# Four input projections of a decoder layer on one core: one 512-column matmul over both parts of x in place of two 256-column passes

## The chip, the cores and the metric

One core of a Trainium2 chip. The metric is the device time of one call in microseconds (us), the median of repeated runs. TensorE, VectorE, ScalarE and GpSimd are called PE, DVE, ACT and POOL, as the profile calls them; SP is the queue that issues most of the DMAs.

## What is computed

A decoder layer for 256 tokens of 1024 channels in float32: RMS norm, one input projection that feeds three branches, a merge with sigmoid gates, an output projection, a squared-ReLU MLP and a final norm. The branches: A is causal attention with 8 heads, B is attention with 8 heads over the 64 keys that an index score selects for each query, C is a short convolution with a gated linear recurrence, multiplied by a GeLU gate.

```python
proj = xn @ w_in
(qa, ka, va, qb, kb, vb, qi, ki, wi, xc, yc, gates) = jnp.split(proj, IN_OFFSETS, axis=-1)
y_a = moba_attention(heads_a(qa), heads_a(ka), heads_a(va), rel_bias[:, :N_HEADS_A])
y_b = dsa_attention(heads_b(qb), heads_b(kb), heads_b(vb), qi, ki, wi, rel_bias[:, N_HEADS_A:])
y_c = rg_lru(causal_depthwise_conv(xc, conv_w, conv_b), ...) * jax.nn.gelu(yc)
# dsa: score[t,s] = sum_h wi[t,h] * relu(qi[t,h] . ki[s]); the 64 best s of each t are kept
x = x + (g0 * (y_a @ w_pa) + g1 * (y_b @ w_pb) + g2 * (y_c @ w_pc)) @ w_o
x = x + jnp.square(jax.nn.relu(rms_norm(x) @ w_up)) @ w_down
```

## The kernel before, in words

Float32 products are made of two rounded parts: every operand is split into a high part (a copy into fp32r by ACT) and the rest (a subtraction by DVE), and a product is three passes, high by high, high by low and low by high. Weights come as 73 tiles of 128x2048, each as two halves of 128x1024; a half is loaded into `raw` (L142), copied into `hi` on ACT (L134) and subtracted into `lo` on DVE (L135). There are five places for `raw` and six each for `hi` and `lo`.

The stages, in the order of the program: index queries, index key and weights (`qi`, `ki`, `wi`) in an order written out by hand (from L327); the index score over 8 heads (L438 to L453) and the selection, eight rounds of MAX8 and MATCH_REPLACE8 for each half of the tokens (L455 to L471); the branch C input `xc` (L506 to L511), its convolution, its gates (`ps_ri`) and the scan; its other input `yc` (L543 to L559); `vb`, `kb`, `qb` and attention B; `va`, `ka`, `qa` and attention A; gates, projections of the branches, `w_o`; the MLP. Outside the parts that are written out by hand, the order of each engine's instructions is made when the kernel is built, by a planner that goes by priorities (program order, unless `tc.high_priority(offset)` puts a block ahead by so many places) and by its own estimate of time; the chip then runs each queue in that fixed order.

Tiles come from pools. All tiles of one tag share that tag's places, and a new tile gets a place when an earlier one is released. The tags that matter here: `acc`, three banks of PSUM of 512 columns, for all projections; `t1`, four places of 128x256, for every temporary of up to 256 columns (`tmp`, L92); `t2`, seven places of 128x512; `u4`, eight places of 128x1024.

In `t1` lie, in program order: some small tiles of the first stage, the rectified index logits `rl` of the first token half (L444), the sixteen tiles `mr` of the selection (L464), and in each attention the tiles `b2` (B only), `z` and `e` of the first token half (L607 to L617). In `t2` lie among others `rl` of the second token half and `y1`, `y2` of the GeLU (L546). In `u4` lie the projected keys and queries, the values, the attention outputs of A, the merged products `mh` and `ml`, and the gain `gf` of the final norm (L775), which is loaded from memory and depends on nothing else.

The projections `xc`, `yc`, `kb`, `qb`, `ka`, `qa` are each 512 features by 256 tokens and are made in two steps `h` of 256 features. A step is `fmajor` (L191): for each chunk of 128 features, three passes of eight matmuls of 256 columns, two chunks side by side in one bank. Then `times` (L416) multiplies the bank by the row `rr` of norm factors on DVE, straight from PSUM, with a high priority. `wide` (L203) is used by the MLP only: eight matmuls of 512 columns (the high weights against both parts of x) and eight of 256 (the low weights against the high part).

`pair_keys` (L255) makes for a pair of heads the copies of the keys: four by ACT, two subtractions and two small copies `keysh` by DVE. `both_parts` (L262) makes two small copies of the queries and two subtractions on DVE. They run once for the index keys (`pair_keys` alone) and once for each of the four pairs of both attentions.

Of the kernel before, what the change touches and what calls it, by code (L numbers as in the profile page):

```python
# [22 lines left out]
AF = mybir.ActivationFunctionType  # L23
# [5 lines left out]
P = 128  # L29
KW = 72  # L30
S = 256
# [20 lines left out]
EVAC = 3000  # L52
# [7 lines left out]
def layer(ctx, tc, x, xf, wts, kiwi, small, wri, rel_bias, onehot, gfin, out):  # L60
    nc = tc.nc
# [15 lines left out]
    def f(ap):  # L77
        return ap.bitcast(F32)

    def acc_tile(name):  # L80
        return pacc.tile([P, 512], F32, tag="acc", name=name)

    def att_tile(name, tag):
        return patt.tile([P, 512], F32, tag=tag, name=name, bufs=1 if tag == "y" else 2)

    def big(name, dt=F32):
        return u4.tile([P, 1024], dt, tag="u4", name=name)

    def side(name, dt=F32):
        return u4.tile([P, 1024], dt, tag="side", name=name, bufs=SIDE)  # L90

    def tmp(name, n, dt=F32):  # L92
        if n <= 256:
            return t1.tile([P, 256], dt, tag="t1", name=name)[:, :n]
        return t2.tile([P, 512], dt, tag="t2", name=name)[:, :n]
# [37 lines left out]
    def split(hi, lo, raw):  # L133
        nc.scalar.activation(hi, raw, AF.Copy)  # L134
        nc.vector.tensor_sub(lo, raw, f(hi))  # L135

    def load(i):

        r = []
        for j in range(2):  # L140
            raw = wp.tile([P, 1024], F32, tag="raw", name=f"raw{i}_{j}", bufs=RAW_BUFS)
            nc.sync.dma_start(raw, wts[i, :, j * 1024:(j + 1) * 1024])  # L142
            r.append((raw, *(wp.tile([P, 1024], F32R, tag=p, name=f"{p}{i}_{j}", bufs=HL_BUFS) for p in ("hi", "lo"))))
        return r
# [4 lines left out]
    def weights():  # L149

        i = next_tile[0]
        next_tile[0] += 1
        if i not in loaded:
            with tc.high_priority(offset=AHEAD):
                loaded[i] = load(i)
                for raw, hi, lo in loaded[i]:
                    split(hi, lo, raw)
        return [w[1:] for w in loaded.pop(i)]
# [32 lines left out]
    def fmajor(ps, w, xx, nk=8, ks=None, cs=(0, 1)):  # L191

        part, ks = ks is not None, ks or range(nk)
        pv = ps.rearrange("p (c t) -> p c t", c=2)
        for c in cs:
            ww = [z.rearrange("p (k c) -> p k c", c=P) for z in w[c]]
            for n, (a, b) in enumerate(PASSES):
                for k in ks:
                    nc.tensor.matmul(pv[:, c, :], ww[a][:, k, :], xx[b][:, k, :],  # L199
                                     start=(n == 0 and k == 0 and (c == 0 or not part)),  # L200
                                     stop=(n == 2 and k == nk - 1 and (c == 1 or not part)))

    def wide(ps, w, x2, ks=range(8)):  # L203

        wh, wl = (z.rearrange("p (k c) -> p k c", c=P) for z in w)
        for k in ks:
            nc.tensor.matmul(ps, wh[:, k, :], x2[:, k], start=(k == 0), stop=False)  # L209
        for k in ks:  # L210
            nc.tensor.matmul(ps[:, :S], wl[:, k, :], x2[:, k, 0], start=False, stop=(k == 7))  # L211
# [12 lines left out]
    xn2 = const.tile([P, 8, 2, S], F32R, name="xn2", tag="xn2")  # L224
    xn = xnh, xnl = xn2[:, :, 0, :], xn2[:, :, 1, :]
# [21 lines left out]
    keys2 = const.tile([P, 2, 2, S], F32R, name="keys2")  # L247
    keysh = const.tile([P, 2, 2, P], F32R, name="keysh")
# [6 lines left out]
    def pair_keys(i, k):  # L255
        for j, r in enumerate(rows):
            for o in rows:
                nc.scalar.activation(keys2[o, i, j, :], k[r], AF.Copy)
            nc.vector.tensor_sub(keysl[r, i, j, :], k[r], f(keys2[r, i, j, :]))
            nc.vector.tensor_copy(keysh[r, i, j, :], f(keys2[r, i, j, :P]))  # L260

    def both_parts(qq, qh, q, scale):  # L262

        for j, r in enumerate(rows):
            nc.vector.tensor_copy(qq[r, j], f(qh[r]))
            nc.vector.scalar_tensor_tensor(qq[rows[1 - j], j], q[r], scale, f(qh[r]), op0=ALU.mult, op1=ALU.subtract)

    ps_q = [acc_tile("ps_qi0"), acc_tile("ps_qi1")]
# [7 lines left out]
    rr = const.tile([P, S], F32, name="rr")  # L276
# [50 lines left out]
    with tc.manual_schedule(engines=ENGINES):  # L327
# [58 lines left out]
        for o in (0, 64):  # L386
            nc.vector.tensor_mul(ki2[o:o + 64], ps_kw[:64, :S], rr[:64])
        pair_keys(0, ki2)
        nc.vector.tensor_copy(wif[64:], ps_kw[64:, :S])

# [22 lines left out]
        nc.vector.tensor_scalar(wi[:, t, :], pt[:, t * 64:t * 64 + 8], r1[t], r1[t], op0=ALU.mult, op1=ALU.mult)  # L413


    def times(dst, ps, row):  # L416

        with tc.high_priority(offset=EVAC):
            nc.vector.tensor_mul(dst, ps.rearrange("p (c t) -> p c t", c=2), row[:, None, :].to_broadcast([P, 2, S]))

    def project_f(name):

        dst = big(name).rearrange("p (c t) -> p c t", c=4)
        for h in range(2):
            ps = acc_tile(f"ps_{name}{h}")
            fmajor(ps, weights(), xn)
            times(dst[:, 2 * h:2 * h + 2, :], ps, rr)
        return dst

    def pair_logits(qh, ql, qq, i, name):  # L430
# [9 lines left out]
    for c in range(4):  # L440
        ls = pair_logits(qi[:, c, :], qil[:, c, :], qiq[:, c], 0, f"i{c}")
        for t in range(2):
# [3 lines left out]
            for j in range(2):  # L446
                h = 2 * c + j
                r = rl[:, j * n:(j + 1) * n]
                w = wi[:, t, h:h + 1]
# [56 lines left out]
    xp = wk.tile([P, 4, S + 3], F32, name="xp", tag="bias")  # L506
    nc.gpsimd.memset(xp[:, :, :3], 0.0)
    for h in range(2):
        ps = acc_tile(f"ps_xc{h}")
        fmajor(ps, weights(), xn)  # L510
        times(xp[:, 2 * h:2 * h + 2, 3:], ps, rr)  # L511
    xc = side("xc").rearrange("p (c t) -> p c t", c=4)
    for c in range(4):
        w = [sp[:, C_CW + 4 * c + i:C_CW + 4 * c + i + 1] for i in range(4)]
# [7 lines left out]
    for c in range(4):  # L522
        ps = att_tile(f"ps_ri{c}", "t")
# [17 lines left out]
        nc.vector.tensor_tensor_scan(hs[:, c, :], av[:, c, :], it[:, c, :], 0.0, op0=ALU.mult, op1=ALU.add)  # L541
    yc = [side("ych", F32R).rearrange("p (c t) -> p c t", c=4), side("ycl", F32R).rearrange("p (c t) -> p c t", c=4)]
    for h in range(2):  # L543
        ps = acc_tile(f"ps_yc{h}")
        fmajor(ps, weights(), xn)
        y1 = tmp(f"y1{h}", 512)  # L546
        y2 = tmp(f"y2{h}", 512)
        times(y1.rearrange("p (c t) -> p c t", c=2), ps, rr)
        nc.scalar.activation(y2, y1, AF.Square)
        nc.vector.tensor_scalar(y2, y2, 0.044715, 1.0, op0=ALU.mult, op1=ALU.add)  # L550
        nc.vector.tensor_mul(y2, y2, y1)
        nc.scalar.activation(y2, y2, AF.Tanh, scale=GELU_C)
        nc.vector.scalar_tensor_tensor(y2, y2, 1.0, y1, op0=ALU.add, op1=ALU.mult)
        hv = hs[:, 2 * h:2 * h + 2, :].rearrange("p c t -> p (c t)")
        nc.vector.scalar_tensor_tensor(y2, y2, 0.5, hv, op0=ALU.mult, op1=ALU.mult)
        ch = yc[0][:, 2 * h:2 * h + 2, :].rearrange("p c t -> p (c t)")
        cl = yc[1][:, 2 * h:2 * h + 2, :].rearrange("p c t -> p (c t)")
        nc.scalar.activation(ch, y2, AF.Copy)
        nc.vector.tensor_sub(cl, y2, f(ch))  # L559
# [21 lines left out]
    def attention(q, k, v, h0, masks, name, pool):  # L581
# [3 lines left out]
        def pair(c):  # L585
            pair_keys(c % 2, k[:, c, :])
            qh, ql = queries(f"qh{name}{c}"), queries(f"ql{name}{c}", 3)
            ql, qq = ql[:, 0], ql[:, 1:]
            nc.scalar.activation(qh, q[:, c, :], AF.Copy, scale=0.125)
            nc.vector.scalar_tensor_tensor(ql, q[:, c, :P], 0.125, f(qh[:, :P]), op0=ALU.mult, op1=ALU.subtract)  # L590
            both_parts(qq, qh[:, P:], q[:, c, P:], 0.125)
            return qh, ql, qq
# [66 lines left out]

    vb = project_v("vb")  # L660
    kb = project_f("kb")
    qb = project_f("qb")
    yb = attention(qb, kb, vb, NH, kmask, "b", const)
    va = project_v("va")
    ka = project_f("ka")
    qa = project_f("qa")
    ya = attention(qa, ka, va, 0, None, "a", u4)
# [55 lines left out]
    for d2 in range(2):  # L723
        mm.append(gate(2, d2))
        w = weights()
# [4 lines left out]
    for d2 in range(2):  # L730
        w = weights()
# [8 lines left out]
    with tc.manual_schedule(engines={ET.PE}):  # L740
        w = weights()
        for t in range(2):
            project(0, 0, t, ya, ga[0], w)
        w = weights()
# [3 lines left out]
        for h in range(2):  # L748
            w = weights()
# [4 lines left out]
        w = weights()  # L754
# [3 lines left out]
        w = weights()  # L758
# [5 lines left out]
        w = weights() + weights()  # L764
# [71 lines left out]
    for t in range(2):  # L836
        v = sm.tile([P, 1], F32, name=f"v2{t}", tag="v")
        nc.vector.tensor_scalar(v, ssq_of(xt[t], f"n2{t}"), 1.0 / DM, EPS, op0=ALU.mult, op1=ALU.add)
        r = tiny_.tile([P, 1], F32, name=f"r2{t}")
# [5 lines left out]
    for t in range(2):  # L845
# [28 lines left out]
        r = sm.tile([P, 1], F32, name=f"rf{t}", tag="rf")  # L874
# [114 lines left out]
```

## Time and profile before

| | |
|---|---|
| median of 3 runs | 450.44 us (449.99 to 450.52) |
| the profiled execution | 450.61 us |
| its span on the core | 448.8 us |
| PE / weight loads / DVE / ACT busy | 98% / 86% / 78% / 60% of the span |
| weights and inputs read | 81.1 MB, 185 GB/s over the span |

The span runs from the first to the last instruction of the core; some 1.8 us of the profiled execution's time lie around it. Busy times of PE are those of pipelined matmuls whose ends are modelled, so the distance from one start to the next says what a matmul costs.

### The profile page before, as it was taken

To read this page: it belongs to the slowest core of one execution; us is meant where nothing else is said; L and a number is where in the kernel's file an instruction comes from. 1 tells how busy PE (TensorE), PEld (TensorE's weight loads), DVE (VectorE), ACT (ScalarE), POOL (GpSimd) and SP (SyncE) were. 2 spreads that over 40 slices of the span, in tenths; PEclk is the share of its full clock that TensorE was granted. 3 is DMA by queue.
4 is the path that set the end of the run, shared out by engine and by line. 5 is a ranking of instruction groups with operands and counts; after the bars stand their busy time and mean duration, and the time that the engine had idled before them with its cause. 6 is when DMAs were issued, how large, how long until landed. Compare 5 with 4: busy or idle time off the path is not lost.

```text
span 448.8 us, 6931 instructions
## 1 busy us (share of the span) xinstructions
PE 440.0 (98%) x2482; PEld 384.8 (86%) x2482; DVE 349.6 (78%) x687; ACT 267.7 (60%) x459; POOL 24.1 (5%) x61
## 2 busy tenths in 40 slices
PE   7999999999999999999999999999999999999994
PEld 7999899989988888888888888888888888888884
DVE  6799999999999999985888587666666666666646
ACT  6848496964467888675644466544444444444453
POOL 4820100000010100000000000000000000000000
PEclk9999999999999999999999999999999999999999
DMA  7998767436764462565555645465665566565202
GB/s 243 371 271 289 251 177 235 144 101 211 236 192 155 140 211 84 192 198 162 188 185 188 229 153 182 149 198 188 195 191 194 191 189 195 187 203 184 85 0 93
DMA packets 23838, 83.39 MB, mean 186 GB/s; under 512 B 2987, under 2 KB 3020, under 8 KB 23804
## 3 DMA queue, kind: packets, MB, share of 16 engines
q1 hardware_dynamic: 22608, 80.00, 54.6%
q0 software_dynamic: 960, 2.88, 2.3%
q8 instruction: 19, 0.31, 0.3%
q14 instruction: 15, 0.12, 0.1%
q10 hardware_dynamic: 236, 0.08, 0.1%
HBM read 81.11 MB, written 1.83 MB: 185 GB/s over the span
## 4 chain that ended last, share of the span: by engine, by line
PE 88%; DMA 4%; POOL 3%; DVE 2%; ACT 1%; issue 1%; SPq 0%; ACTq 0%; DVEq 0%; POOLq 0%
PE pd L815 19%; PE ps_g L219 15%; PE ps_up L209 13%; PE ps_p L219 7%; PE ps_up L211 7%; PE po L219 5%; DMA raw<-wts 3%; PE ps_qa L199 3%; PE ps_qb L199 3%; PE ps_kb L199 3%; PE ps_ka L199 3%; PE ps_va L219 2%; PE ps_vb L219 2%; DVE lo L135 1%; DMA x<-xf 1%
## 5 line engine op out<-in xcount | busy, mean ns | idle before, releaser
L135 DVE TENSOR_TENSOR lo<-raw,hi 128x1024 fp32r<-128x1024 f32 (+1 forms) x146 | 174.5, 1207 | 59.1 <-ACT hi L134 58.6
L134 ACT ACTIVATE hi<-raw 128x1024 fp32r<-128x1024 f32 (+1 forms) x146 | 149.8, 1045 | 93.1 <-issue 19.6
L209 PE MATMUL ps_up<-x,hi 128*128 128x512 f32 x256 | 64.7, 393 | 0.2 <-DVE x L186 0.2
L209 PEld LDWEIGHTS ps_up<-x,hi 128*128 128x128 f32 x256 | 46.7, 188 | 9.3 <-DVE x L186 0.4
L219 PE MATMUL ps_g<-hi,xn 128*128 128x512 f32 x192 | 53.7, 392 | 0.0
L815 PE MATMUL pd<-hi,hl 128*128 128x512 f32 (+1 forms) x128 | 49.5, 387 | 0.0
L815 PE MATMUL pd<-lo,hh 128*128 128x512 f32 (+1 forms) x128 | 49.4, 386 | 0.0
L815 PE MATMUL pd<-hi,hh 128*128 128x512 f32 (+1 forms) x128 | 49.1, 387 | 0.0
L219 PEld LDWEIGHTS ps_g<-hi,xn 128*128 128x128 f32 x192 | 35.6, 188 | 6.8
L211 PEld LDWEIGHTS ps_up<-x,lo 128*128 128x128 f32 x256 | 35.3, 190 | 2.7
L211 PE MATMUL ps_up<-x,lo 128*128 128x256 f32 x256 | 36.2, 282 | 0.0
L219 PE MATMUL ps_g<-lo,xn 128*128 128x512 f32 x96 | 30.2, 392 | 0.0
L815 PEld LDWEIGHTS pd<-lo,hh 128*128 128x128 f32 x128 | 24.0, 188 | 5.0
L815 PEld LDWEIGHTS pd<-hi,hh 128*128 128x128 f32 x128 | 24.0, 188 | 4.5
L815 PEld LDWEIGHTS pd<-hi,hl 128*128 128x128 f32 x128 | 24.1, 188 | 4.4
L802 ACT ACTIVATE hh<-z 128x512 fp32r<-128x512 f32 x16 | 10.1, 631 | 29.1 <-DVE z L800 29.1
L219 PEld LDWEIGHTS ps_g<-lo,xn 128*128 128x128 f32 x96 | 17.9, 188 | 3.6
L803 DVE TENSOR_TENSOR hl<-z,hh 128x512 fp32r<-128x512 f32 x16 | 11.1, 691 | 9.8 <-ACT hh L802 9.8
L168 POOL TENSOR_TENSOR ssq_n<-q_n 128x1 f32<-128x1 f32 x2 | 0.4, 192 | 277.6 <-ACT scr_n L166 277.6
L796 DVE TENSOR_TENSOR z<-ps_up,u 128x256 f32<-128x256 f32 x32 | 13.4, 418 | 0.0
L684 ACT ACTIVATE g<-ps_g,rh 128x512 f32<-128x512 f32 x12 | 8.2, 684 | 7.0 <-PE ps_g L219 7.0
L795 ACT ACTIVATE u<-ps_up 128x256 f32<-128x256 f32 x32 | 11.8, 368 | 0.0
(344 smaller groups left out, 777.1 us busy)
## 6 DMA issues: line engine op xcount, KB each, us to landing
raw<-wts SPq DMA_DIRECT2D x142, 512.0 KB, 4.8
x<-xf SPq DMA_DIRECT2D x4, 256.0 KB, 4.7
raw<-wts SPq DMA_DIRECT2D x4, 256.0 KB, 4.5
x<-x SPq DMA_DIRECT2D x2, 512.0 KB, 5.0
biasb<-toep POOLq DMA_DIRECT2D x8, 128.0 KB, 6.5
biasa<-toep POOLq DMA_DIRECT2D x8, 128.0 KB, 2.7
out<-o SPq DMA_DIRECT2D x2, 512.0 KB, 2.6
toep<-rrow POOLq DMA_DIRECT2D x1, 766.0 KB, 6.5
```

The costliest lines, as they stand in the source:

```text
L134: nc.scalar.activation(hi, raw, AF.Copy)
L135: nc.vector.tensor_sub(lo, raw, f(hi))
L199: nc.tensor.matmul(pv[:, c, :], ww[a][:, k, :], xx[b][:, k, :], start=(n == 0 and k == 0 and (c == 0 or not part)), stop=(n == 2 and k == ...
L209: nc.tensor.matmul(ps, wh[:, k, :], x2[:, k], start=(k == 0), stop=False)
L211: nc.tensor.matmul(ps[:, :S], wl[:, k, :], x2[:, k, 0], start=False, stop=(k == 7))
L219: nc.tensor.matmul(ps, xx[b][:, k0 + k, d], ww[a][:, k, :], start=(first and n == 0 and k == 0), stop=(last and n == 2 and k == nk - 1))
L684: nc.scalar.activation(g[:, t, :], ps, AF.Tanh, scale=rh[:, t:t + 1])
L795: nc.scalar.activation(u, ps[:, S:], AF.Copy)
L796: nc.vector.tensor_add(z[:, d], ps[:, :S], u)
L802: nc.scalar.activation(hh, z, AF.Copy)
L803: nc.vector.tensor_sub(hl, z, f(hh))
L815: nc.tensor.matmul(ps, hid[g][b][:, c, d], w_down[g][c][a][:, s], start=(g == (NG - LAG if o else 0) and c == 0 and m == 0), stop=(g == NG ...
```

## The change

`fmajor` and `times` of six projections are replaced by `chunks`: for each chunk of 128 features one bank is filled by `wide`; ACT copies the bank's second half into a temporary `u` of 256 columns, DVE adds the first half to it into the destination, and after two chunks DVE multiplies 512 columns of the destination by `rr` in place. `u` is a `tmp` of 256 columns, so it lies in `t1`. The small copies in `pair_keys` and `both_parts` go from DVE to ACT.

```diff
             nc.vector.tensor_sub(keysl[r, i, j, :], k[r], f(keys2[r, i, j, :]))
-            nc.vector.tensor_copy(keysh[r, i, j, :], f(keys2[r, i, j, :P]))
+            nc.scalar.activation(keysh[r, i, j, :], f(keys2[r, i, j, :P]), AF.Copy)
...
-            nc.vector.tensor_copy(qq[r, j], f(qh[r]))
+            nc.scalar.activation(qq[r, j], f(qh[r]), AF.Copy)
...
-    def times(dst, ps, row):
-
+    def chunks(name, h, dst):
+
+        w = weights()
+        for c in range(2):
+            ps = acc_tile(f"ps_{name}{h}{c}")
+            wide(ps, w[c], xn2)
+            u = tmp(f"u_{name}{h}{c}", S)
+            with tc.high_priority(offset=EVAC):
+                nc.scalar.activation(u, ps[:, S:], AF.Copy)
+                nc.vector.tensor_add(dst[:, c, :], ps[:, :S], u)
         with tc.high_priority(offset=EVAC):
-            nc.vector.tensor_mul(dst, ps.rearrange("p (c t) -> p c t", c=2), row[:, None, :].to_broadcast([P, 2, S]))
+            nc.vector.tensor_mul(dst, dst, rr[:, None, :].to_broadcast([P, 2, S]))
...
-            ps = acc_tile(f"ps_{name}{h}")
-            fmajor(ps, weights(), xn)
-            times(dst[:, 2 * h:2 * h + 2, :], ps, rr)
+            chunks(name, h, dst[:, 2 * h:2 * h + 2, :])
...
-        ps = acc_tile(f"ps_xc{h}")
-        fmajor(ps, weights(), xn)
-        times(xp[:, 2 * h:2 * h + 2, 3:], ps, rr)
+        chunks("xc", h, xp[:, 2 * h:2 * h + 2, 3:])
...
-        ps = acc_tile(f"ps_yc{h}")
-        fmajor(ps, weights(), xn)
         y1 = tmp(f"y1{h}", 512)
         y2 = tmp(f"y2{h}", 512)
-        times(y1.rearrange("p (c t) -> p c t", c=2), ps, rr)
+        chunks("yc", h, y1.rearrange("p (c t) -> p c t", c=2))
```

## Rows read from the trace of the kernel before

**Rows 1.** The page: busy times of the engines; granted clock in 40 slices.

```profile
PE 440.0 (98%) x2482; PEld 384.8 (86%) x2482; DVE 349.6 (78%) x687; ACT 267.7 (60%) x459; POOL 24.1 (5%) x61
PEclk9999999999999999999999999999999999999999
```

**Rows 2.** PE's waits: line, waited for, us in total, times, longest.

```profile
PE ps_qi L343 <- ACT hi L134: 1.4, 1, 1.4
PE ps_up L209 <- DVE x L186: 0.2, 1, 0.2
```

**Rows 3.** A stretch: its length, busy PE, PEld, DVE, ACT, POOL, clock, DMA, GB/s.

```profile
20.00:205.00 185.00, 184.87 (x1164) 167.05 (x1164) 176.85 (x443) 132.68 (x250) 11.20 (x22) 1.00 0.61 194
```

**Rows 4.** The chain that ended last: start, length, what.

```profile
99.48 11.51 PE ps_ka L199 x96
...
274.83 1.84 PE ps_up L209 x8
276.67 0.95 PE ps_up L211 x8
```

**Rows 5.** Groups by line and shape: busy us, mean ns of one, idle before.

```profile
L135 DVE TENSOR_TENSOR lo<-raw,hi 128x1024 fp32r<-128x1024 f32 x142 | 171.7, 1221 | 58.8 <-ACT hi L134 58.3
...
L796 DVE TENSOR_TENSOR z<-ps_up,u 128x256 f32<-128x256 f32 x32 | 13.4, 418 | 0.0
L795 ACT ACTIVATE u<-ps_up 128x256 f32<-128x256 f32 x32 | 11.8, 368 | 0.0
L803 DVE TENSOR_TENSOR hl<-z,hh 128x512 fp32r<-128x512 f32 x16 | 11.1, 691 | 9.8 <-ACT hh L802 9.8
L260 DVE CAST keysh<-keys 64x128 fp32r<-64x128 f32 x18 | 3.9, 217 | 0.1
```

**Rows 6.** `t2`: yc's matmuls, the write of `y1`, the last `rl`.

```profile
41.03 1.12 PE L199 MATMUL ps_yc<-xn,lo 128*128 128x256 f32 x8
...
L419 DVE TENSOR_TENSOR y<-ps_yc,rr x2: 692/692/693, 54.7 to 56.0; 128x512 f32<-128x512 f32 x2
...
55.07 0.60 ACT L445 ACTIVATE rl<-l_i 128x512 f32<-128x512 f32 x1 [2.59 <-PE l_i L437]
```

**Rows 7.** `u4`: `gf` is loaded, and `ml` written (first and last start).

```profile
L776 SPq DMA_DIRECT2D gf<-gfin x1: 424/424/424, 247.6 to 247.6; - x1
L704 DVE SCALAR_TENSOR_TENSOR ml<-ps_m,mh x4: 683/684/691, 239.0 to 251.0; 128x512 fp32r<-128x512 f32 x4
```

**Rows 8.** `t1` in attention B: `e` of pair 1 (ACT), `b2` of pair 2 (DVE).

```profile
137.11 0.39 ACT L620 ACTIVATE eb<-zb,nmb 128x128 f32<-128x128 f32 x1
137.60 0.42 DVE L608 TENSOR_TENSOR b2b<-biasb,score 128x256 f32<-128x256 f32 x1
```

**Rows 9.** DVE: the last round of the selection begins; the mask behind it.

```profile
124.69 0.61 DVE L466 MAX8 m<-mr 128x8 f32<-128x128 f32 x2
125.87 0.42 DVE L471 TENSOR_SCALAR score<-mr 128x128 f32<-128x128 f32 x2
```

**Rows 10.** `xc`'s fourth chunk on PE; index weights and one score head on DVE.

```profile
32.06 2.08 PE L199 MATMUL ps_xc<-xn,hi 128*128 128x256 f32 x16
42.99 0.48 DVE L413 TENSOR_SCALAR wi<-pt_wi,r 128x8 f32<-128x8 f32 x2
51.49 0.74 DVE L453 SCALAR_TENSOR_TENSOR score<-rl,wi,score 128x128 f32<-128x128 f32 x2
```

**Rows 11.** Attention B: queries leave PSUM; its first logits; `e` of its last pair.

```profile
L419 DVE TENSOR_TENSOR qb<-ps_qb,rr x2: 672/678/684, 84.0 to 91.8; 128x512 f32<-128x512 f32 x2
127.14 0.28 DVE L613 CUSTOM_DVE_ANT_0 zb<-l_b,b2b 128x128 f32<-128x128 f32 x1
157.92 0.40 ACT L620 ACTIVATE eb<-zb,nmb 128x128 f32<-128x128 f32 x1 [0.24 <-DVE nmb L616]
```

**Rows 12.** The end of attention A (DVE), and its first reader (PE).

```profile
L657 DVE TENSOR_TENSOR yla<-ya,yha x8: 406/418/428, 200.8 to 227.4; 64x256 fp32r<-64x256 f32 x8
L219 PE MATMUL ps_p<-hi,yla x16: 389/389/397, 229.7 to 239.9; 128*128 128x512 f32 x16
```

## The prediction

> **What bounds the kernel now.** I read first the page's busy line and clock slices [rows 1]: PE is busy for 98% of the span at the upper of its two clock levels throughout, DVE for 78%, ACT for 60%. Busy PE is no proof, so the list of PE's waits comes next [rows 2]: past the first microseconds it waits for nothing worth counting, 0.2 us at the start of the MLP. The matmuls follow each other at one step per shape for the whole span; a microsecond taken from PE's stream is a microsecond of the span, and so is one in which PE must stand. The chain of waits says the same and gives the steps [rows 4]: 96 matmuls of 256 columns in 11.51 us (119.9 ns each), eight of 512 in 1.84, eight of 256 in 0.95.
>
> Then I looked for what stands close behind. From 20 to 205 us DVE is busy for 176.85 of 185 us [rows 3], so 8.1 us are free there. All six projections of the change lie in this stretch. Last I looked at which tile gets a buffer when, since the change adds 24 tiles to a tag with four places, and that decides my forecast.
>
> **The change, part by part.** PE: a chunk of 128 features costs 24 x 0.1199 = 2.88 us now and 1.84 + 0.95 = 2.79 us in the new form, the same number of columns but 16 weight loads for 24. That is 0.088 us for each of 24 chunks, 2.1 us in all, if PE keeps streaming.
>
> The Trainium skill speaks against even this: "TensorE: Matmul & The Clock Gate", Back-to-back issue gap, gives N/2.4 + 2.5 ns, so 24 x 109.2 = 2.62 us now against 8 x 215.8 + 8 x 109.2 = 2.60 after, an estimate of 0.5 us in all. The trace has 119.9 ns for 256 columns [rows 4], more than the page, and the measurement decides.
>
> DVE: 24 additions of 256 columns from PSUM at 418 ns come in, 10.0 us; the twelve multiplications stay, at 691 ns for 512 columns from SBUF against 692 from PSUM [rows 5, 6]; 18 + 16 small copies leave at 217 ns (the queries' copies have the same 64x128 shape), 7.4 us. Net +2.6 us. ACT: 24 copies from PSUM at 368 ns, 8.8 us, and 34 small copies between 0.22 us (DVE's price) and 0.39 us (128x128 on ACT [rows 8]), 7 to 13 us; ACT has 52 us free from 20 to 205 [rows 3], and that hides them. In front of later ACT work a copy waits at most its own length; I cost it at nothing, and at those 0.4 us if the next weight half is due.
>
> PSUM: a bank holds one chunk instead of two, so the three places cover 8.4 us of PE's work instead of 17.3. A bank is now free only when a `u` has a place in `t1`, ACT has copied and DVE has added.
>
> So, **when does `u` get a place?** Three rows say that the places of a tag are given in program order, even if a later tile is ready and places are free. First, `gf`: its load depends on nothing, and of the eight places of `u4` only `ml` and `mh` and the two outputs of A are taken at the end; yet it is issued at 247.6 us, between the first and last writes of `ml`, the last tiles of that tag ahead of it in the program [rows 7]. Second, `y1`: the matmuls of its first half are done by 42.2 us and its multiplication has the highest priority, yet it runs at 54.7, next to the first use of the fourth `rl` of `t2` at 55.07, the tile just before it in program order; the second `y1` follows at 56.0 [rows 6]. Third, `b2` of attention B needs only a bias and the mask, which is there at 126.3; pair 2's runs at 137.60, just behind the first use of pair 1's `e` at 137.11, the tile before it in `t1` [rows 8, 9].
>
> In `t1` the sixteen `mr` tiles of the selection stand ahead of the first `u` of `xc`. If order holds, no chunk of `xc` can leave PSUM before the last `mr` has its place, that is, before the last round of the selection, which now runs until 125.9 beside everything else. PE fills three banks and stands; `yc`, `vb` and all later projections need the same banks. What PE can do meanwhile are the index logits, 20 matmuls of 256 columns and 4 of 512: 20 x 0.12 + 4 x 0.23 = 3.3 us.
>
> How long it stands: the index weights are ready at 42.99 now; two multiplications of 0.69 us leave DVE's queue ahead of them, so 41.6. Eight heads at 0.74 us [rows 10] make 5.9, scaling about 0.5, and eight rounds at 125.87 - 124.69 = 1.18 us [rows 9] 9.4: 57.4. The copy and the addition, 0.37 + 0.42 and about 0.2 of hand-over, give 58.4. DVE is otherwise nearly empty there, for without PE no place for split weights comes free; up to three splits of 1.22 us [rows 5] may still lie in between, so 62 at most. At the other end the weights could be ready 3 us earlier: 55. The fourth chunk starts at 32.06 now [rows 10]. So 58.4 - 32.1 = 26.3, less 3.3 of logits done meanwhile, less 21 x 0.088 = 1.8 still to be gained: **+21.2 us** (17.8 to 24.8).
>
> The same again for `ka`: its `u` stands behind all `b2`, `z` and `e` of attention B. From the fourth chunk of `xc` to three quarters of `ka` PE needs 99.48 + 8.6 - 32.1 = 76.0 us now [rows 4, 10], less 3.3 and 16 x 0.088: 71.3, so it would reach that point at 129.7, or at about 137 with three pairs of B done beside it (each 8 x 0.12 + 4 x 0.23 + 6 transposes of at most 0.12 = 2.6). B can start when the first queries are out of PSUM, now 84.0 [rows 11], then 58.4 + 51.9 - 4.3 = 106, and 4 to 10 us of copies and logits later. From its first logits to the last pair's `e` it takes 157.92 - 127.14 = 30.8 us now [rows 11], with a full DVE; with the score and selection gone from DVE perhaps three quarters. That is 133 to 147, so PE stands 0 to 10 us; I take 4.
>
> Together +25.2 us. The profiled execution took 450.61 us (span 448.8), so 475.8; the median lies 0.2 below it: **475.6**, with 466 to 487 as this case's own range (17.8 and nothing, less 2 for what I don't see; 24.8 and 10, and a little more).
>
> The Trainium skill adds a cost that no row here can price: by "TensorE: Matmul & The Clock Gate", Part 1, an idle TensorE falls back to the lower of its two clock levels and starts there again. The clock slices of before show only the upper level; nothing for it is in the sum.
>
> **The rivals.** (1) Places go to whoever is ready: then nothing holds `u`, PE streams on, and the 2.1 us are gained: 448.3. For it: PE has no wait now, ACT has room, and the MLP evacuates its banks in just this way beside a PE that does not wait [rows 2, 5]. Against it: the three rows above, and DVE's 8.1 us. With the page's gap formula the same case would end at 450. Chance 0.15. It decides at the first `u`: copied while the selection still runs, or not.
>
> (2) Places are free, but DVE becomes the bound. It gets 2.6 us more, and up to 125 us nearly all of the additions with only a third of the relief. The end of attention A is close: its last `yla` is written at 227.8, PE reads it first at 229.7 [rows 12], 1.8 us of slack. PE arrives 2.1 earlier, DVE up to 2.6 later: PE stands 2.1 + 2.6 - 1.8 = 2.9, and the net is +0.8: 451.3. If DVE's free 8.1 us absorb the additions it is 449.5, and if banks that now turn over twice as fast also make PE wait at `yc`, up to 455. Chance 0.20, half of it beyond +0.2%.
>
> (3) The order holds, but the planner finds less to stand for: a selection that is done by 50, for instance, would give 467, which the range of my case has in it. If the order holds for some tags only, the case is one of the first two.
>
> **How the numbers follow.** The forecast has 0.63, rivals 1 and 2 0.15 and 0.20, and 0.02 is left for something else. A measurement of this kernel can tell about 0.2% (0.9 us) from no change. Slower: 0.63 + 0.10 = 0.73 and 0.01 of the rest; same: 0.10 of rival 2 and 0.02 of rival 1, 0.12; faster: 0.13 and 0.01, 0.14. My own case covers about 0.57 by its range; to hold 8 in 10 the range must take in rival 2 and the edge of rival 1, so it goes from 449 to 487.
>
> **What would show it.** In the profile after, if I am right: the rounds of the selection follow each other in about 1.2 us each and end before 62; the first ACT copy out of `ps_xc` comes right behind them; PE's slices are thin between 31 and 58; PE's waits name DVE or ACT at `ps_xc`; the clock slices may dip; from 60 on everything looks as before, 21 to 25 us later, perhaps with a second gap in `ka`. The PE step is right if eight matmuls of 512 and eight of 256 take 2.79 us in `ps_xc`. I am wrong about the order of places if a `u` of `xc` is copied at 26 to 40 while `mr` rounds still run at 70 or later; wrong about the size if the score ends much before 47 or its rounds are split by other DVE work.

## The result, and the profile after

The changed kernel takes 488.5 us (median of 6 runs, 486.9 to 491.5), the kernel before 450.5 beside it: a ratio of 1.0845, 95% interval 1.0826 to 1.0863. The forecast was 475.6, with 449 to 487 as the stated range; the result lies 1.5 us above its upper end. The profiled execution of the changed kernel took 486.9 us, its span is 484.9.

The page of after, against [rows 1]. The first line is busy time, the two others are PE's busy share and its granted clock in 40 slices of 12.1 us:

```profile
PE 447.8 (92%) x2290; PEld 381.2 (79%) x2290; DVE 354.2 (73%) x677; ACT 287.1 (59%) x517; POOL 24.1 (5%) x61
PE   8948099989968999999999999999999999999995
PEclk9987599999988999999999999999999999999999
```

PE has 192 matmuls fewer (2290 for 2482), but two holes: slices 3 to 5 (24 to 61 us) and slices 12 and 13 (133 to 158). In both the granted clock falls. Behind them the stream is as dense as before. PE's waits, against [rows 2] (line, waited for, us in total, times, longest):

```profile
PE ps_xc L209 <- DVE xp L425: 12.5, 1, 12.5
PE l_i L440 <- ACT keysh L260: 7.0, 1, 7.0
PE yb L649 <- ACT p0hb L642: 3.2, 1, 3.2
PE t0b L635 <- DVE p0lb L643: 2.0, 1, 2.0
PE ps_qb L209 <- DVE kb L425: 1.8, 1, 1.8
```

The timeline of the two holes (start, length, what, and in brackets how long the engine sat idle before and what released it):

```profile
38.93 3.71 PE L209 MATMUL ps_xc<-xn,hi 128*128 128x512 f32 x8
...
58.70 1.05 ACT L424 ACTIVATE u_xc<-ps_xc 128x256 f32<-128x256 f32 x3 [10.80 <-DVE mr L474]
...
58.91 0.42 DVE L477 TENSOR_SCALAR score<-mr 128x128 f32<-128x128 f32 x2
59.25 1.08 DVE L425 TENSOR_TENSOR xp<-ps_xc,u_xc 128x256 f32<-128x256 f32 x3
...
59.72 3.57 PE L209 MATMUL ps_xc<-xn,hi 128*128 128x512 f32 x8 [12.46 <-DVE xp L425]
...
110.73 2.00 PE L209 MATMUL ps_qb<-xn,hi 128*128 128x512 f32 x8
112.57 1.12 PE L211 MATMUL ps_qb<-xn,lo 128*128 128x256 f32 x8
113.52 1.09 PE L219 MATMUL ps_va<-hi,xn 128*128 128x512 f32 x4
...
146.41 0.40 ACT L622 ACTIVATE eb<-zb,nmb 128x128 f32<-128x128 f32 x1 [0.31 <-DVE nmb L618]
...
146.81 0.36 ACT L424 ACTIVATE u_ka<-ps_ka 128x256 f32<-128x256 f32 x1
...
148.68 3.45 PE L209 MATMUL ps_ka<-xn,hi 128*128 128x512 f32 x8
```

The first two chunks of `xc` were done before 30 us and the third at 43.6, and nothing left their banks before 58.70, released by the last `mr`. The wait of 7.0 us at the index logits lies inside the same hole: it ended at 36.7, before the third chunk. The fourth chunk follows at 59.72 (32.06 before, [rows 10]). In the second hole ACT copies `u` of `ka` at once behind the first `e` of attention B's last pair, its predecessor in `t1`. Where PE streams, a chunk takes 113.52 - 110.73 = 2.79 us, as forecast.

The clock, by windows (length; busy PE, PEld, DVE, ACT, POOL; granted clock; DMA share; GB/s), against [rows 3]:

```profile
36.00:60.00 24.00, 10.40 (x43) 8.07 (x44) 20.27 (x77) 7.47 (x15) 0.00 (x0) 0.64 0.35 131
...
64.00:130.00 66.00, 64.19 (x348) 55.48 (x347) 58.75 (x105) 53.66 (x100) 4.32 (x8) 1.00 0.50 160
130.00:153.00 23.00, 16.52 (x81) 13.56 (x81) 21.22 (x74) 18.03 (x55) 2.20 (x5) 0.85 0.55 160
```

In the stretches in which PE stood, part of its work ran at the lower of the two levels (1.2 GHz), and so did most of the chunk behind each hole: eight matmuls of 512 columns took 3.57 and 3.45 us (granted clock 0.53 and 0.55) instead of 2.00. The third chunk of `xc`, behind the wait at the logits, took 3.71 (0.51). The Trainium skill ("TensorE: Matmul & The Clock Gate", Part 1) has an idle TensorE fall back to the lower level and start there again; the trace agrees in these three places.

### The profile page after: what moved, and what is told of

It reads as the page before. It is cut to its first block, busy times and chain, and to the rows that moved or that the text cites. A ratio compares the mean times of both kernels' runs of the same rounds, so it can differ in the third digit from the quotient of the medians.

```text
span 484.9 us, 6610 instructions
## 1 busy us (share of the span) xinstructions
PE 447.8 (92%) x2290; PEld 381.2 (79%) x2290; DVE 354.2 (73%) x677; ACT 287.1 (59%) x517; POOL 24.1 (5%) x61
## 3 DMA queue, kind: packets, MB, share of 16 engines
q0 software_dynamic: 960, 2.88, 2.1%
## 4 chain that ended last, share of the span: by engine, by line
PE 82%; DVE 6%; ACT 6%; DMA 4%; issue 1%; SPq 0%; DVEq 0%; ACTq 0%
PE pd L817 18%; PE ps_g L219 14%; PE ps_up L209 12%; PE ps_p L219 7%; PE ps_up L211 6%; PE po L219 5%; DMA raw<-wts 3%; PE ps_vb L219 2%; ACT hi L134 2%; PE ps_va L219 2%; PE ps_yc L209 2%; PE ps_kb L209 2%; PE ps_qa L209 2%; PE ps_xc L209 1%; PE ps_qi L199 1%
## 5 line engine op out<-in xcount | busy, mean ns | idle before, releaser
L219 PE MATMUL ps_g<-hi,xn 128*128 128x512 f32 x192 | 52.4, 392 | 0.0
L817 PEld LDWEIGHTS pd<-lo,hh 128*128 128x128 f32 x128 | 24.1, 188 | 4.9
L817 PEld LDWEIGHTS pd<-hi,hl 128*128 128x128 f32 x128 | 24.1, 188 | 4.4
L209 PE MATMUL ps_xc<-xn,hi 128*128 128x512 f32 x32 | 11.4, 514 | 12.5 <-DVE xp L425 12.5
L209 PEld LDWEIGHTS ps_xc<-xn,hi 128*128 128x128 f32 x32 | 7.8, 257 | 14.8 <-DVE xp L425 12.8
```

Source lines behind the costliest of these rows:

```text
L219: nc.tensor.matmul(ps, xx[b][:, k0 + k, d], ww[a][:, k, :], start=(first and n == 0 and k == 0), stop=(last and n == 2 and k == nk - 1))
L817: nc.tensor.matmul(ps, hid[g][b][:, c, d], w_down[g][c][a][:, s], start=(g == (NG - LAG if o else 0) and c == 0 and m == 0), stop=(g == NG ...
```

## The experiments

The theory on trial: places of a tag are handed out in program order, so `u` waits for tiles of other stages. Its rivals: places go to whoever is ready and DVE or ACT is simply too busy; or banks that turn over twice as fast make PE wait in any case.

### The first and the second stop, one at a time

The selection's tiles in another tag, everything else as in the changed kernel:

```diff
-            nxt = [tmp(f"mr{t}{i}", P * (t + 1)) for t in range(2)]
+            mr = prob(f"mr{i}", 512, F32)
+            nxt = [mr[:, :P], mr[:, P:P + S]]
```

> The changed kernel with one edit: the tiles of the selection lie in another tag, so that no tile of the selection stands ahead of u in t1. Theory (places are given in program order): the first u of xc is copied right after its chunk, at 26 to 30 us, while the selection's rounds still run later; PE does not stop at xc. The second cause is still there: u of ka stands behind attention B's tiles, and B now ends late because the selection again runs beside everything else (mask at 126 us in the kernel before). PE would reach three quarters of ka at about 107 to 114 us and stand until the last e of B, 137 to 158, with some 8 us of B's own PE work done meanwhile: 14 to 30 us over the time before, 465 to 480. Rival A (places go to whoever is ready and the stop at xc has another cause, such as DVE or ACT being busy): 485 to 490, with the stop at xc unchanged. Rival B (only the selection's tiles mattered, the second stop had another cause): 448 to 455.

478.5 us, 1.059 of before (1.054 to 1.064); the profiled execution was the fastest of four, 474.2. The timeline of ACT in this run, and the selection's row in the view of the tile `mr` (shortest, median and longest duration in ns; first and last start):

```profile
44.65 0.88 ACT L451 ACTIVATE rl<-l_i 128x512 f32<-128x512 f32 x2 [0.41 <-PE l_i L443]
45.40 0.67 ACT L424 ACTIVATE u_xc<-ps_xc 128x256 f32<-128x256 f32 x2
...
136.15 0.40 ACT L623 ACTIVATE eb<-zb,nmb 128x128 f32<-128x128 f32 x1 [1.19 <-DVE nmb L619]
...
136.66 0.38 ACT L424 ACTIVATE u_ka<-ps_ka 128x256 f32<-128x256 f32 x1
```

```profile
L473 DVE MAX8 m<-mr x14: 279/342/416, 56.1 to 92.8; 128x8 f32<-128x128 f32 x7, 128x8 f32<-128x256 f32 x7
```

`u` of `xc` is now copied before the selection's later rounds, which run until 93; so `mr` had held it. But it is copied at 45.4 and not at 26 to 30: I had overlooked the next tiles in `t1`, the index logits `rl` of the first token half (the row at 44.65 holds one `rl` of each half, the smaller one last). The second stop is there and longer: PE fills its banks at `ka` 14.7 us earlier than in the changed kernel (121.8 for 136.5), while the first `e` of attention B's last pair comes only 10.3 us earlier (136.15 for 146.41).

Attention B behind `va`, `ka`, `qa` in program order, `mr` in its old place:

```diff
-    yb = attention(qb, kb, vb, NH, kmask, "b", const)
     va = project_v("va")
     ka = project_f("ka")
     qa = project_f("qa")
+    yb = attention(qb, kb, vb, NH, kmask, "b", const)
```

> The changed kernel with one edit: attention B stands behind the projections va, ka and qa in program order, so that no tile of B stands ahead of u of ka in t1; the selection's tiles still stand ahead of u of xc. Theory (places in program order): the stop at xc is as in the changed kernel, until about 59 us; there is none at ka. The net of the second stop was about 10 us plus the lower clock behind it, so 488.5 becomes 474 to 481. Rival A (the second stop comes from ACT or DVE being late with B whatever the order): 485 to 490. Rival B (what is lost after the first stop is the clock and DVE): above 481.

477.0 us, 1.058 (1.056 to 1.061). PE's waits in this run keep the first stop and have none at `ka`:

```profile
PE ps_xc L209 <- DVE xp L425: 12.5, 1, 12.5
PE l_i L440 <- ACT keysh L260: 7.0, 1, 7.0
PE ps_qb L209 <- DVE kb L425: 1.8, 1, 1.8
```

So the second stop is worth 488.5 - 477.0 = 11.5 us, and the first stop with everything else that the change brings 477.0 - 450.7 = 26.3.

Both edits together, and the same two edits in the kernel before:

> The changed kernel with both edits: the selection's tiles in another tag and attention B behind va, ka and qa in program order. Theory: PE stops nowhere between 20 and 130 us, and what is left is the change itself: 447 to 449 if PE streams to the end (450.5 less 2.1), 450 to 453 if DVE's extra 2.6 us come to bear at the end of attention A or at a bank of PSUM. Rival (the stops come from DVE or ACT not keeping up with banks that turn over twice as fast): 460 or more, with waits of PE on the addition spread over xc to qa.

> The kernel before with the same two edits (the selection's tiles in another tag, attention B behind va, ka and qa in program order). It tells what the edits cost or give by themselves, so that e3_both can be compared with it. All theories: 449.5 to 453; PE waits for nothing in the projections, as in the kernel before. If it is slower, the difference between e3_both and this one is the worth of the change without the stops: theory -2 to +2 us.

The control has 450.4 us (0.9992, 0.998 to 1.000): the edits cost nothing by themselves. With the change they give 462.1 (1.024, 1.021 to 1.027), not 447 to 453 but in the rival's range. Yet the waits are not spread as the rival has them. The one long wait is at the index logits, and `u` of `xc` is copied at 48.3, behind the last `rl` of the first half (PE's waits, then ACT's timeline):

```profile
PE l_i L440 <- ACT keysh L260: 9.1, 1, 9.1
```

```profile
47.54 0.87 ACT L451 ACTIVATE rl<-l_i 128x512 f32<-128x512 f32 x2 [0.41 <-PE l_i L443]
48.30 0.67 ACT L424 ACTIVATE u_xc<-ps_xc 128x256 f32<-128x256 f32 x2
```

### u where nothing stands ahead of it

```diff
-            u = tmp(f"u_{name}{h}{c}", S)
+            u = prob(f"u_{name}{h}{c}", S, F32)
```

`u` now lies in `p1`, two places, used otherwise by the attentions. First alone, then with attention B behind:

> The changed kernel with one edit: u lies in p1, the tag of attention's second transposed probabilities, where neither the selection's nor the index logits' tiles stand ahead of it; in the program only attention B's tiles of that tag stand between qb and ka. Theory (places in program order; in the run with the selection's tiles elsewhere it was the index logits rl of the first half that still held u until 48 us): u of xc is copied within 1 us of its chunk, at 26 to 30, with no stop at xc at all; the stop at ka stays, since B's tiles still stand ahead of ka's u. If the end of B is set by when its queries come, the stop is as long as with the selection's tiles elsewhere and the time is about 14 us under that run's 478.5, 464 to 470; if DVE's work sets B's end, PE only comes earlier to the same stop: 473 to 479. Rival (u of xc was held by something other than its place): a stop at xc until about 48 us again.

> The changed kernel with u in p1 and attention B behind va, ka and qa: no tile that is released late stands ahead of any u. Theory (places were the whole loss): PE waits nowhere between 20 and 130 us; 447 to 449 if PE streams to the end, 450 to 453 if DVE's net 2.6 us come to bear. Rival A (banks that turn over twice as fast make PE wait for ACT and DVE even with places free): 454 to 462, with waits of 1 to 3 us on the addition in each projection. Rival B (the small copies on ACT stand behind weight copies that wait for their load): a stop of 5 to 9 us at the first index logits, and 455 to 460.

Alone: 483.4 us (1.072, 1.069 to 1.074), more than I expected. There is no stop at `xc` beyond 3.0 us, but the one at `ka` is the longest of all. Its `e` and its `u` (the first from the view of the tile `eb`, the second from ACT's timeline):

```profile
L622 ACT ACTIVATE eb<-zb,nmb x16: 385/447/507, 117.5 to 137.8; 128x128 f32<-128x128 f32 x8, 128x256 f32<-128x256 f32 x8
```

```profile
148.11 0.66 ACT L424 ACTIVATE u_ka<-ps_ka 128x256 f32<-128x256 f32 x2 [2.75 <-PE yb L653]
```

In `p1` the tiles ahead of `u` are not `e` but the transposed probabilities of B's last pair, which come free only when PE has read them: 148.1 instead of 137.8. The same rule, with a later predecessor.

With attention B behind: 461.2 us (1.023, 1.020 to 1.025). Now no `u` stands behind tiles of another stage; still the time is 10.5 us over before, in the range of rival A. PE's waits in this run, and a piece of its timeline:

```profile
PE ps_xc L209 <- DVE xp L425: 3.0, 1, 3.0
PE ps_va L219 <- DVE qb L425: 2.4, 1, 2.4
PE ps_ri L532 <- DVE xcl L135: 1.4, 1, 1.4
```

```profile
26.53 0.38 ACT L424 ACTIVATE u_xc<-ps_xc 128x256 f32<-128x256 f32 x1 [0.57 <-PE ps_xc L211]
...
30.31 1.21 DVE L135 TENSOR_TENSOR lo<-raw,hi 128x1024 fp32r<-128x1024 f32 x1
31.55 0.87 DVE L387 TENSOR_TENSOR ki<-ps_kw,rr 64x256 f32<-64x256 f32 x2
32.45 0.43 DVE L425 TENSOR_TENSOR xp<-ps_xc,u_xc 128x256 f32<-128x256 f32 x1
...
32.93 3.46 PE L209 MATMUL ps_xc<-xn,hi 128*128 128x512 f32 x8 [3.01 <-DVE xp L425]
```

The copy is there at 26.53, 0.57 us after the chunk, the addition only at 32.45: DVE's queue has splits and `ki` ahead of it. Of the three banks the third still holds the index key `ps_kw`, read by `ki` at 31.55 and by the index weights later, so two chunks fill what is free and PE stands 3.0 us; most of the chunk behind runs at the lower clock (0.57 granted), 3.46 us for 2.00.

### The small copies

In the kernel before alone, and taken back in the run above:

```diff
-            nc.vector.tensor_copy(keysh[r, i, j, :], f(keys2[r, i, j, :P]))
+            nc.scalar.activation(keysh[r, i, j, :], f(keys2[r, i, j, :P]), AF.Copy)
...
-            nc.vector.tensor_copy(qq[r, j], f(qh[r]))
+            nc.scalar.activation(qq[r, j], f(qh[r]), AF.Copy)
```

> The kernel before with only the small copies of keys and queries moved to ACT; the projections are as before. If the copies are hidden on ACT, as the prediction had it at no cost: 449.5 to 451. If a copy stands behind a weight copy that waits for its load and PE waits for it at the logits: 452 to 458, with a wait of PE on keysh or the queries' copy.

> The run before this one (u in p1, attention B behind) with the small copies of keys and queries back on DVE. DVE has 34 x 0.217 = 7.4 us more, ACT 10 us less. If DVE bounds: 2 to 5 us slower than with the copies on ACT. If the copies on ACT stand behind waiting weight copies and hold the logits: faster by up to 5 us or more. If neither: within 1 us of it.

450.5 us (0.9995, 0.998 to 1.001), and 460.4 against 461.2, within the scatter. In these two kernels the copies are worth nothing either way: some 6 us more or less of DVE's busy time (349.6 and 343.6, 356.9 and 351.0) move nothing, so the sum of DVE's work by itself isn't what holds PE. With `u` in `p1` and B behind, PE has no wait at the logits, so a copy on ACT that stands behind a weight copy waiting for its load (rival B) costs nothing there. In the changed kernel itself the second `keysh` did run behind such a copy, which had waited 0.88 us; what that adds to the stop at `xc` was not separated.

### What holds the rest: additions, banks, GpSimd

Three edits of the run with 461.2 us: ACT copies the first half of the bank instead of DVE adding it; the twelve multiplications on GpSimd; the old matmuls, but one bank for each chunk.

```diff
-                nc.vector.tensor_add(dst[:, c, :], ps[:, :S], u)
+                nc.scalar.activation(dst[:, c, :], ps[:, :S], AF.Copy)
```

> The run with u in p1 and attention B behind (461.2 us, 10.5 over before though every u finds a place at once), with the addition left out: ACT copies the first half of the bank straight into the destination and the second half into u, which nobody reads; DVE is rid of 24 x 0.42 = 10.0 us and no bank waits for DVE any more. Part of the computation is missing (the low parts of x). If the remaining 10.5 us are banks held until DVE's queue comes to the addition: 447 to 450, no wait of PE on xp or qb. If they are the banks turning over twice as fast for any evacuation, or DVE's other work (xcl ahead of the gates): 455 to 461.

```diff
-            nc.vector.tensor_mul(dst, dst, rr[:, None, :].to_broadcast([P, 2, S]))
+            nc.gpsimd.tensor_mul(dst, dst, rr[:, None, :].to_broadcast([P, 2, S]))
```

> The run with u in p1 and attention B behind, with the twelve multiplications by the row of norm factors on GpSimd (it reads and writes SBUF only there): DVE is rid of 12 x 0.69 = 8.3 us, the additions stay. If DVE's amount of work holds PE: 450 to 455. If only the place of the additions in DVE's queue does (an addition behind two or three splits of 1.2 us while two or three banks are full): 457 to 462. GpSimd's time for 128x512 is not in any trace here; where the result is needed soon (keys, xc), a slow one costs, up to 465.

```diff
-            wide(ps, w[c], xn2)
-            u = prob(f"u_{name}{h}{c}", S, F32)
+            fmajor(ps, [w[c]], xn, cs=(0,))
...
-                nc.scalar.activation(u, ps[:, S:], AF.Copy)
-                nc.vector.tensor_add(dst[:, c, :], ps[:, :S], u)
-        with tc.high_priority(offset=EVAC):
-            nc.vector.tensor_mul(dst, dst, rr[:, None, :].to_broadcast([P, 2, S]))
+                nc.vector.tensor_mul(dst[:, c, :], ps[:, :S], rr)
```

> The run with u in p1 and attention B behind, with the old form of the matmuls (24 of 256 columns for a chunk) but still one bank for each chunk, multiplied by the norm factors straight from the bank (256 columns on DVE); no u and no addition. PE's gain of 2.1 us is undone, DVE has 24 x 0.42 in place of 24 x 0.42 + 12 x 0.69. If a bank for each chunk is enough to make PE wait for DVE: 455 to 461. If the step through ACT and the extra DVE work make the loss: 450 to 452.

One bank for each chunk with the old matmuls: 455.8 us (1.012, 1.010 to 1.014), and PE's only wait in the projections is the one at `xc`:

```profile
PE ps_xc L199 <- DVE xp L423: 3.0, 1, 3.0
```

Half the loss of the 461.2 comes without any addition, from the bank for each chunk. GpSimd: 464.5 us (1.031, 1.030 to 1.033), slower. The twelve multiplications take 1.28 to 3.69 us there (0.68 to 0.69 on DVE in the changed kernel), and the keys come later. PE's longest wait, the longest multiplication, and the subtractions of B's keys on DVE (shortest, median, longest in ns):

```profile
PE ps_qb L209 <- DVE qb L425: 3.3, 1, 3.3
```

```profile
91.37 3.69 POOL L427 TENSOR_TENSOR kb<-kb,rr 128x512 f32<-128x512 f32 x1 [4.88 <-DVE kb L425]
```

```profile
L259 DVE TENSOR_TENSOR keysl<-kb,keys x8: 403/420/1356, 91.2 to 134.0; 64x256 fp32r<-64x256 f32 x8
```

DVE was not relieved: its busy time is 353.8 us, against 351.0 with the multiplications on it, and single instructions beside GpSimd's took up to 3.2 times as long. So this run doesn't tell what less work on DVE would give.

Without the additions: 454.7 us (1.008, 1.006 to 1.010; the profiled execution took 457.2), between the two cases that I had named. PE waits at `yc` for ACT, and the rows of the tiles `y` and `rl` say why:

```profile
L425 ACT ACTIVATE y<-ps_yc x4: 365/390/414, 54.1 to 59.5; 128x256 f32<-128x256 f32 x4
```

```profile
L451 ACT ACTIVATE rl<-l_i x8: 369/494/619, 46.1 to 53.6; 128x256 f32<-128x256 f32 x4, 128x512 f32<-128x512 f32 x4
```

No DVE in between, and yet the first write of `y` comes right behind the last `rl`. That points to the order of places again, in `t2`, where `y1` stands behind the index logits of the second half. It is the very pair that [rows 6] show.

### The stops at xc and yc

`xc` in the old form, the rest as in the run with 461.2; then `xc` and `yc` in the old form; then all but `ka` and `qa`:

```diff
-        chunks("xc", h, xp[:, 2 * h:2 * h + 2, 3:])
+        ps = acc_tile(f"ps_xc{h}")
+        fmajor(ps, weights(), xn)
+        times(xp[:, 2 * h:2 * h + 2, 3:], ps, rr)
```

> The run with u in p1 and attention B behind (461.2 us), with xc alone in the old form: two chunks to a bank, multiplied straight from it; yc, kb, qb, ka, qa in the new form. When xc starts, one of the three banks still holds the index key and weights, and with a bank for each chunk the other two were full at 29.9 us, three microseconds before DVE came to them. If that stop and the lower clock behind it are worth 5 us: 455 to 457, no wait of PE at xc. If the additions merely meet a full DVE, wherever they are: 459 to 461.

> The same with xc and yc in the old form; kb, qb, ka, qa in the new one (16 chunks: PE -1.4 us, DVE +6.7 us of additions in the stretch from 63 to 122 us). If the loss is the additions in DVE's queue behind the splits, these four keep half to two thirds of it: 452 to 455, with PE waiting for DVE at qb or va. If the loss was in the first stages alone: 448.5 to 450.

> The same with only ka and qa in the new form (8 chunks: PE -0.7 us, DVE +3.3 us from 99 to 122 us). If DVE catches up behind 122 us before PE needs it: 449 to 450.5, the best of these kernels; if the additions cost here as elsewhere: 451 to 453.

459.8 us (1.019, 1.016 to 1.022), 451.5 (1.002, 1.000 to 1.004) and 450.2 (0.999, 0.998 to 1.000). The first lies where I had put a DVE that is full wherever the additions fall (459 to 461). The stop at `xc` is gone there, and PE only comes earlier to the next one (timeline of ACT and DVE):

```profile
50.55 0.60 ACT L456 ACTIVATE rl<-l_i 128x512 f32<-128x512 f32 x1 [0.67 <-PE l_i L448]
...
52.39 0.74 DVE L425 TENSOR_TENSOR y<-ps_yc,u_yc 128x256 f32<-128x256 f32 x2
```

Three chunks of `yc` were done by 44.7 and left their banks from 52.39 on. To tell the place from a full DVE, `y1` in another tag, with `xc` in the new and in the old form:

```diff
-        y1 = tmp(f"y1{h}", 512)
+        y1 = prob(f"y1{h}", 512, F32)
```

> The run with u in p1 and attention B behind (461.2 us), and y1, the destination of yc's chunks, in p2 instead of t2, where it stands behind the index logits of the second token half. In that run no chunk of yc left its bank before the last of these logits had its place (54.1 us; additions at 55.0), and yc's fourth chunk began at 55.49, two microseconds of waiting and of work drawn forward later than the third ended. If the order of places is the cause there too: the additions of yc follow their chunks within 1 to 3 us from 45 on, PE does not stop at the gates or yc, and the time is 456 to 459 (the stop at xc, worth 1.4 to 5, and those at qb and va stay). If a full DVE is the cause: 460 to 462, with the additions of yc no earlier than 52.

> The same, with xc in the old form besides (459.8 us with y1 in t2). With neither the stop at xc nor the one at yc, what is left is the additions in DVE's queue at yc, kb, qb, ka and qa: 451 to 455 if the two stops were most of the rest, since the run with xc and yc in the old form has 451.5; 457 to 460 if DVE holds PE up in any case.

458.5 us (1.016, 1.012 to 1.020) and 452.6 (1.005, 1.003 to 1.007). The additions of `yc` no longer wait for the logits (the first from DVE's timeline with `xc` in the new form, the second with `xc` in the old one; the last `rl` starts at 55.7 and 58.9 there):

```profile
48.42 0.42 DVE L425 TENSOR_TENSOR y<-ps_yc,u_yc 128x256 f32<-128x256 f32 x1
```

```profile
45.23 0.41 DVE L425 TENSOR_TENSOR y<-ps_yc,u_yc 128x256 f32<-128x256 f32 x1
```

The two stops hide each other: one alone gives 1.4 (`xc`, within the scatter) or 2.7 us (`yc`), both 461.2 - 452.6 = 8.6. The remaining 2 us over before are not taken apart; in the profiled execution, the slowest of nine at 455.6, PE waits 1.8 us at the index logits and 1.6 at `ka`.

The edits in order, each with those above it, medians:

| | us |
|---|---|
| the changed kernel | 488.5 |
| attention B behind `va`, `ka`, `qa` | 477.0 |
| `mr` elsewhere | 462.1 |
| `u` in `p1` in place of that | 461.2 |
| `y1` in `p2` | 458.5 |
| `xc` in the old form | 452.6 |
| the kernel before | 450.5 |

No version is measurably faster than the kernel before. With `ka` and `qa` alone 8 x 0.088 = 0.7 us should be gained; the medians are 450.2 and 450.4 (control), within their scatter, so the gain is not shown in the time. With `kb` and `qb` besides, PE waits 0.9 us for the addition of `ka` and 0.7 at `ka` itself, more than the 16 x 0.088 = 1.4 that the step gives.

## Why the prediction was right in kind and too small

**PE's step** (2.88 to 2.79 us a chunk): right in the trace of after; no time shows it, since every version that has it also waits or lies within the scatter.

**The small copies** at nothing: right where it was tried; 305 ns each on ACT, between the bounds of 0.22 and 0.39.

**Places in program order**: right, and now shown by moving the tiles. `u` followed `mr`, then `rl` when `mr` was gone, then its own chunk when both were.

**The first stop**, +26.3 us to the fourth chunk of `xc`: it measured 59.72 - 32.06 = 27.7. But the term of +21.2 us (17.8 to 24.8), with all that follows, became 26.3 (the run without the second stop). Three terms failed. The stop ended 1.3 us later than forecast: the eight rounds took the 9.4 us of the forecast, but the index score before them 8.9 (from 40.1 to 49.0) instead of 5.9, since PE ran the third chunk at the lower clock ahead of the later logits, and the 1.5 us by which it began earlier did not make up for it. The clock, left at nothing in the sum: 3.57 for 2.00 us behind the stop, 1.6. And **the bank that holds one chunk, costed at nothing**: I wrote down that three banks now cover 8.4 us instead of 17.3 and gave it no price; `qb` waited 1.8 us for `kb`'s addition, as much as the remaining gain that I had subtracted. Together 1.3 + 1.6 + 1.8 = 4.7 of the 5.1; no run takes the three apart.

**The second stop**, 4 us taken from 0 to 10: 11.5 by experiment, outside its bounds. PE filled its banks at 136.5 (forecast about 137). From attention B's first `z` to the first `e` of its last pair it took 146.4 - 122.3 = 24.1 us, 0.78 of the 30.8 before, so "perhaps three quarters" held. The step that failed is the start of B: the first queries were to be out of PSUM at 58.4 + 51.9 - 4.3 = 106, which leaves their evacuation as it was. Before, and then after (timelines of PE and DVE):

```profile
80.79 1.12 PE L199 MATMUL ps_qb<-xn,lo 128*128 128x256 f32 x8
```

```profile
104.90 1.11 PE L211 MATMUL ps_qb<-xn,lo 128*128 128x256 f32 x8
...
108.82 0.42 DVE L425 TENSOR_TENSOR qb<-ps_qb,u_qb 128x256 f32<-128x256 f32 x1
...
111.49 0.42 DVE L425 TENSOR_TENSOR qb<-ps_qb,u_qb 128x256 f32<-128x256 f32 x1
...
113.89 0.68 DVE L427 TENSOR_TENSOR qb<-qb,rr 128x512 f32<-128x512 f32 x1
...
122.33 0.28 DVE L615 CUSTOM_DVE_ANT_0 zb<-l_b,b2b 128x128 f32<-128x128 f32 x1
```

Before, the multiplication followed its two chunks after 2.1 us (81.9 to 84.0, [rows 11]); after, two copies, two additions and the multiplication stand in the queues of ACT and DVE between `kb`'s work and the splits, and it followed after 7.9 (106.0 to 113.9). So B's first `z` came at 122.3 and not at 110 to 116. That the longer evacuation made B late is read from this trace; no run changes it alone. The lower clock behind the stop adds 1.45 us. The second stop is the larger part of the miss: 7.5 of 12.9 us.

**The rivals.** With every place of `u` free I forecast 448.3 (places free) or 449.5 to 455 (DVE the bound); the run has 461.2. Both prices left out that two of three banks were free at `xc`, and that `y1` stands behind `rl` in `t2`. The second I had in my own rows, as evidence for the rule, and did not apply it to the change: before, the two `yc` banks could wait until 54.7 us because each held two chunks and the third bank was enough for `vb`. With both out of the way (and `xc` in the old form) the time is 452.6, inside the range of the second rival.

## What to carry to other kernels

Before a temporary goes into a shared tag, list every tile that stands ahead of it there, and when the last of them is released; do the same for the tag of the destination, and for every tag that is moved to. When an accumulator holds half as much work, the evacuation's slack halves too: look up for each stage how many banks are really free and how late the evacuation was before. When a step of evacuation becomes three, ask what waits for its result: the queries here came 5.8 us later behind their matmuls. A gain of 2 us on the bounding engine is soon outweighed by one wait of 3.

## What was not expected of the hardware

The clock's fall is not only a matter of long stops: after a wait of 3.0 us at `xc` eight matmuls of 512 columns took 3.46 us instead of 2.00 (granted clock 0.57), so that a wait of 3 us cost about 4.5. After a wait of 1.8 us (`xc` old, `y1` elsewhere) four 512-column matmuls took 1.91 us instead of 1.07 (granted clock 0.50); behind the 1.8 us at `qb` in the changed kernel eight took 2.11 (clock 1.00), hardly more than without a wait. So the length of the wait just before does not by itself tell whether the clock falls.

On GpSimd the multiplication of 128x512 took 1.28 to 3.69 us, against 0.68 to 0.69 on DVE, and DVE's instructions beside it took longer: a subtraction of 64x256 up to 1.36 us instead of 0.42. DVE's busy time rose by 2.8 us though twelve of its instructions had left it.
